# Two-layer diffusion backbone on one core: the modulation vectors of a half step are summed over the partitions in one pair of products at its end

## Chip, cores and metric

One Trainium2 chip, one of its cores. The metric is device time of one execution in microseconds (us); a difference is told against the runs of the kernel before on the same chip.

## What is computed

A two-layer block over 512 latent tokens and 256 context tokens of width 1024. Each layer is a half-step FFN, a token mixer (windowed attention in layer 0, Fourier mixing in layer 1), and a second half-step FFN. Every sub-layer is modulated by three vectors (shift, scale, gate) that come from a conditioning vector `c` through a large matrix. The part of the reference that matters:

```python
def modulate(x, mod, j):
    shift, scale = mod[:, 3 * j], mod[:, 3 * j + 1]
    return x * (1 + scale[:, None, :]) + shift[:, None, :]

def post_norm_update(x, y, mod, j, g, b):
    gate = mod[:, 3 * j + 2][:, None, :]
    return layer_norm(ALPHA * x + gate * y, g, b)

def half_ffn_sublayer(x, mod, j, wi, wo, g, b):
    y = 0.5 * swiglu(modulate(x, mod, j), wi, wo)
    return post_norm_update(x, y, mod, j, g, b)

mod_lat = (silu(c) @ mod_w[i] + mod_b[i]).reshape(-1, 9, D_MODEL)      # latent stream
mod_ctx = (silu(c_ctx) @ mod_w[i] + mod_b[i]).reshape(1, 9, D_MODEL)   # context stream
```

So nine vectors of 1024 for each layer and stream; vector 3j is the shift, 3j+1 the scale, 3j+2 the gate of sub-layer j. All arithmetic is fp32 in effect.

## The kernel before, in words

**Products.** Each fp32 factor is split into two parts of the fast fp32 format, high and low: ScalarE copies the high part (`wh`, `uh`, `hh`), VectorE subtracts to get the low one (`wl`, `ul`, `hl`). A product is then three matmuls (`mm3`: high-high, low-high, high-low).

**A half step** (`half_step`) has two stages. In the *up* stage (`ffn_up`) 22 pairs p = 0..21 are worked through; pair p computes two 128-row halves, `up` for the gate (silu on ScalarE: `sg`) and `up` for the value (VectorE multiplies: `u`). For 512 tokens a pair is 48 matmuls of 512 columns, for the 256 context tokens 48 of 256. In the *down* stage (`project`) the 22 rows of the down weights are worked through, f = 0..21; for each f four token tiles of six matmuls into `y`. There are eight PSUM banks, taken in turn: a pair takes two, a token tile of `y` two, a modulation product (`mp`) one. Five half steps run: 1 latent, 2 context (both layer 0, before attention), 3 latent (layer 0, after attention), 4 latent (layer 1, before the Fourier mixer), 5 latent (layer 1, after it).

**The gate** of a half step is folded into its down weights: `wr<-wr,gr` on VectorE multiplies each raw row block by `gr`, the gate as a row broadcast to all partitions. `gate_row` makes it, called from `late()` ahead of pair 20: ScalarE scales the column form (`gs`), its queue issues a DMA that writes it to DRAM as 1024 single numbers (`there`, called *the scatter* below) and, when that has landed, a DMA that reads it back broadcast (`gr`, called *the fetch*). Both stand in ScalarE's own instruction stream, which goes on behind the fetch only when the scatter has landed.

**The modulation vectors** beyond the first two are made beside the up stages of half steps 1 to 4 on VectorE: for each vector and stream eight steps `acc<-mr,silu_c,acc` over row blocks `mr` of the matrix, then `mod_fold`: a 32x32 transpose and a reduction that leave 128 partial sums in 32 columns. `mod_reduce` sums these over the partitions: one fp32 matmul with the constant `folder` into `mp`, and four small adds of the bias into `mod`. It is called for each vector a few steps after its fold (MOD_LAG), and for what is left in `mod_finish`, behind pair 19. Half step 1 makes the vectors shift/scale/gate 0 of the context, gate 0 of the latents, and 3 and 4 of both (8 products), half step 2 vectors 5 to 7 (3), half step 3 vector 8 (its own gate) and 0 to 3 of layer 1 (5), half step 4 vectors 4 to 8 of layer 1 (5; vector 5 is the Fourier mixer's gate, fetched in the same `late()` as the half step's own).

**What sets the order.** TensorE's and GpSimd's instructions stay in program order. VectorE's, ScalarE's and the DMA queue's (SP) are ordered by a scheduler when the kernel is built, except in stretches that are pinned; once built, each engine's stream is fixed. Raw weights come over SP, all through 42 SBUF slots. Completion of DMAs is counted on eight counters in turn, SP's and ScalarE's together: a DMA on a counter waits for the one eight before it.

Of the kernel before, what the change touches and what calls it, by code (L numbers as in the profile page):

```python
# [10 lines left out]
F32 = mybir.dt.float32  # L11
F32R = mybir.dt.float32r
AF = mybir.ActivationFunctionType
ALU = mybir.AluOpType

P = 128
D = 1024
KC = D // P
BLK = 32
# [29 lines left out]
P_WIDTH = 648  # L49
CORE_FETCH = 6  # L50
CORE_TILES = 5
MOD_LAG = 3
MOD_EARLY = 1
TURN_ACT = 4
BETWEEN = 5
# [49 lines left out]
class Emitter:  # L105
# [110 lines left out]
    def mod_fold(self, l, v, s, a):  # L216


        nc = self.nc
        turned = self.slot([P, 1024], F32, "mt")  # L220
        nc.vector.transpose(turned, a)
        t = self.small([P, D // BLK], "mr")
        nc.vector.tensor_reduce(
            out=t, in_=turned.rearrange("p (c k) -> p c k", k=BLK), axis=mybir.AxisListType.X, op=ALU.add
        )
        return l, v, s, t

    def mod_reduce(self, l, v, s, t):
        nc = self.nc
        ps = self.bank(nm="mp")  # L230
        self.mm(ps[:, : D // BLK], self.folder, t, start=True, stop=True)
        per = P // BLK
        for q in range(per):
            rows = slice(q * BLK, (q + 1) * BLK)
            cols = slice(v * KC, (v + 1) * KC)
            nc.vector.tensor_tensor(
                self.mod[l][s][rows, cols], ps[rows, q : D // BLK : per], self.mod_b[l][rows, cols], ALU.add
            )

    def mod_steps(self, n, ahead=2):  # L240
        nc = self.nc
        for _ in range(n):
            if self.n_job >= len(self.jobs):
                break
            while self.n_mraw < min(self.n_job + ahead + 1, len(self.jobs)):
                l, v, _, k = self.jobs[self.n_mraw]
                r = self.slot([P, 1024], F32, "mr")
                nc.sync.dma_start(r, self.ins["mod_w"][l, v, k])
                self.mraw[self.n_mraw] = r
                self.n_mraw += 1  # L250
            l, v, streams, k = self.jobs[self.n_job]
            r = self.mraw.pop(self.n_job)
            self.n_job += 1
            while self.due and self.due[0][0] <= self.n_job:
                self.mod_reduce(*self.due.pop(0)[1])
            for s in streams:
                sc = self.silu_c[:, s, k : k + 1]
                if k == 0:
                    a = self.slot([P, 1024], F32, "acc")
                    self.acc[s] = a  # L260
                    nc.vector.tensor_scalar(a, r, sc, None, ALU.mult)
                else:
                    a = self.acc[s]
                    nc.vector.scalar_tensor_tensor(a, r, sc, a, ALU.mult, ALU.add)
                if k == KC - 1:
                    self.due.append((self.n_job + MOD_LAG, self.mod_fold(l, v, s, self.acc.pop(s))))

    def mod_finish(self, upto):
        if upto > self.n_job:
            self.mod_steps(upto - self.n_job)  # L270
        while self.due:
            self.mod_reduce(*self.due.pop(0)[1])

    def col(self, l, s, v):
        return self.mod[l][s][:, v * KC : (v + 1) * KC]
# [492 lines left out]
    def run(self):  # L768
        nc = self.nc
        ins = self.ins  # L770
        sync = nc.sync
# [40 lines left out]

        h, held = self.head()
        sync.dma_start(self.mod_b[1], ins["mod_b"][1])
        self.folder = self.const([P, P], F32, "folder")
        sync.dma_start(self.folder, ins["folder"])
        self.ln_g = self.const([P, 6 * KC], F32, "ln_g")
        self.ln_b = self.const([P, 6 * KC], F32, "ln_b")
        sync.dma_start(self.ln_g, ins["ln_g_col"])
# [1 line left out]
        x = []  # L821
# [627 lines left out]
```

## Time and profile before

| | us |
|---|---|
| runs | 1991.20 median of 3 (1990.84 to 1992.42) |
| profiled execution | 1992.59, of it span 1990.8 |
| TensorE busy | 1971.8 (99% of the span), 10124 matmuls |
| VectorE busy | 1277.0 (64%) |
| ScalarE busy | 681.2 (34%) |
| DMA | 296.27 MB, mean 149 GB/s |

The page gives the busy time of each engine over the span; the chain gives, followed back from the last instruction, who was waited for. Busy times here mix stages: what a wait costs is read in the stage where it stands. In rows of the timeline the first number is the start, the second the length of a piece, `x2` how many like instructions are merged, and the bracket at the end the idle time before it and what ended that.

### The profile page before, as it was taken

The page shows a single profiled execution, that of the slowest core. Times are in us where ns is not written, and L with a number is a line of the kernel's source. Part 1 is how long each engine was busy: PE and PEld are TensorE (multiplying, and loading weights), DVE is VectorE, ACT ScalarE, POOL GpSimd, SP SyncE. Part 2 cuts the span into 40 slices and gives each one's busy share as a digit, 9 for nine tenths or more (in the row PEclk, how much of TensorE's full clock was granted, in tenths as well). Part 3 has the DMA queues.
Part 4 walks back from the last instruction along what each step waited for, and adds up shares of the span by engine and source line. Part 5 has one row for each costly group of instructions (what it writes and reads, how often), then busy time and mean ns, then how long its engine had stood idle before and what let it go on. Part 6 is the DMA issues. An engine that isn't in the chain of part 4 may idle for free.

```text
span 1990.8 us, 25353 instructions
## 1 busy us (share of the span) xinstructions
PE 1971.8 (99%) x10124; PEld 1674.7 (84%) x10124; DVE 1277.0 (64%) x1713; ACT 681.2 (34%) x991; POOL 73.4 (4%) x138
## 2 busy tenths in 40 slices
PE   8999999999999999999999999999999999999998
PEld 7888888899888887988888888888888988888886
DVE  6569985598756775766658455664766873333744
ACT  3322243334533685422224232222333632212320
POOL 0000000000000460000000000000000000000000
PEclk9999999999999999999999999999999999999999
DMA  9756543388732013455543326554441333232411
GB/s 377 262 185 206 185 150 131 116 297 297 254 101 73 10 45 107 159 190 196 195 149 123 120 98 225 195 191 138 140 135 64 110 98 117 90 94 87 138 64 43
DMA packets 90198, 296.27 MB, mean 149 GB/s; under 512 B 17248, under 2 KB 17504, under 8 KB 90080
## 3 DMA queue, kind: packets, MB, share of 16 engines
q1 hardware_dynamic: 81792, 290.96, 43.0%
q10 hardware_dynamic: 8288, 3.70, 0.7%
q8 instruction: 79, 1.29, 0.3%
q14 instruction: 39, 0.32, 0.1%
HBM read 292.50 MB, written 2.13 MB: 148 GB/s over the span
## 4 chain that ended last, share of the span: by engine, by line
PE 96%; DVE 2%; DMA 1%; ACT 1%; issue 0%; DVEq 0%; POOL 0%; SPq 0%; ACTq 0%; POOLq 0%
PE up L72 54%; PE y L72 30%; PE qkv L72 4%; PE s L72 2%; PE pt L72 2%; PE o L72 1%; PE tp L72 1%; DVE wl L72 1%; DVE x L72 0%; PE ab L72 0%; DMA wr<-in_wi_head_dram 0%; PE qt L72 0%; DVE ul L72 0%; PE f L72 0%; DMA ln_b<-in_ln_b_col_dram 0%
## 5 line engine op out<-in xcount | busy, mean ns | idle before, releaser
L72 DVE TENSOR_TENSOR wl<-wr,wh 128x1024 fp32r<-128x1024 f32 (+1 forms) x359 | 429.1, 1217 | 90.9 <-ACT wh L72 55.3
L72 ACT CAST wh<-wr 128x1024 fp32r<-128x1024 f32 (+1 forms) x364 | 368.5, 1046 | 218.2 <-PE y L72 92.5
L72 PE MATMUL up<-hh,wh 128*128 128x512 f32 (+1 forms) x1152 | 429.6, 373 | 0.0
L72 PE MATMUL up<-hl,wh 128*128 128x512 f32 (+1 forms) x1152 | 428.3, 372 | 0.0
L72 PE MATMUL up<-hh,wl 128*128 128x512 f32 (+1 forms) x1152 | 428.1, 372 | 0.0
L72 PE MATMUL y<-wh,uh 128*128 128x512 f32 x920 | 302.7, 390 | 1.4 <-DVE oT L72 1.4
L72 ACT ACTIVATE sg<-up 128x512 f32<-128x512 f32 (+1 forms) x110 | 61.1, 555 | 703.5 <-PE up L72 703.5
L72 PE MATMUL y<-wh,ul 128*128 128x512 f32 x920 | 301.8, 389 | 0.0
L72 PE MATMUL y<-wl,uh 128*128 128x512 f32 x920 | 301.6, 389 | 0.0
L72 DVE TENSOR_TENSOR u<-up,sg 128x512 f32<-128x512 f32 (+1 forms) x110 | 70.1, 637 | 335.0 <-PE up L72 334.6
L72 PEld LDWEIGHTS up<-hl,wh 128*128 128x128 f32 x1152 | 217.1, 188 | 37.5
L72 PEld LDWEIGHTS up<-hh,wl 128*128 128x128 f32 x1152 | 217.2, 189 | 37.2
L72 PEld LDWEIGHTS up<-hh,wh 128*128 128x128 f32 x1152 | 217.2, 189 | 36.9
L72 PEld LDWEIGHTS y<-wh,uh 128*128 128x128 f32 x920 | 172.6, 188 | 37.1 <-DVE oT L72 1.8
L72 PEld LDWEIGHTS y<-wh,ul 128*128 128x128 f32 x920 | 172.8, 188 | 35.9
L72 PEld LDWEIGHTS y<-wl,uh 128*128 128x128 f32 x920 | 172.8, 188 | 35.5
L72 DVE SCALAR_TENSOR_TENSOR acc<-mr,silu_c,acc 128x1024 f32<-128x1024 f32 x147 | 186.1, 1280 | 1.4
L72 DVE TENSOR_TENSOR wr<-wr,gr 128x1024 f32<-128x1024 f32 x99 | 120.5, 1238 | 41.4 <-DMA wr<-in_wo_dram 22.3
L72 PE MATMUL up<-h0h,wh 128*128 128x512 f32 x352 | 139.1, 398 | 0.2 <-ACT h0h L72 0.2
L72 PE MATMUL up<-h0l,wh 128*128 128x512 f32 x352 | 136.4, 390 | 0.0
L72 PE MATMUL up<-h0h,wl 128*128 128x512 f32 x352 | 136.2, 390 | 0.0
L72 PE MATMUL up<-chh,wh 128*128 128x256 f32 x352 | 100.1, 284 | 0.0
(171 smaller groups left out, 2143.0 us busy)
## 6 DMA issues: line engine op xcount, KB each, us to landing
wr<-in_wi_dram SPq DMA_DIRECT2D x213, 512.0 KB, 4.4
mr<-in_mod_w_dram SPq DMA_DIRECT2D x144, 512.0 KB, 4.1
wr<-in_wo_dram SPq DMA_DIRECT2D x110, 512.0 KB, 3.9
m<-in_mod_head_dram SPq DMA_DIRECT2D x16, 512.0 KB, 8.1
wr<-in_wqkv_dram SPq DMA_DIRECT2D x12, 512.0 KB, 3.6
wr<-in_attn_wo_dram SPq DMA_DIRECT2D x8, 512.0 KB, 3.5
wr<-in_fourier_wo_dram SPq DMA_DIRECT2D x8, 512.0 KB, 3.5
wr<-in_wi_head_dram SPq DMA_DIRECT2D x8, 448.0 KB, 9.6
```

Source lines behind the costliest of these rows:

```text
L72: ins = f(*args, **kw)
```

## The change

The vectors of a half step are no longer summed over the partitions one by one. Each fold writes its partial sums into a common tile `sums`; behind pair 19 one call splits the whole tile into high and low (`mp`, 32 columns for each vector: 256, 96, 160 and 160 columns in half steps 1 to 4), two matmuls with `folder`, now in the fast fp32 format, add both parts up, and the bias is added for runs of neighbouring vectors at once. So 21 products of one vector become 4 times 2, and 84 bias adds 28. `MOD_LAG` goes. `folder` is loaded into a slot and copied by ScalarE.

```diff
-MOD_LAG = 3
+MOD_MOST = 8
...
         nc.vector.transpose(turned, a)
-        t = self.small([P, D // BLK], "mr")
+        if not self.due:
+            self.sums = self.pool.tile([P, MOD_MOST, D // BLK], F32, tag="sums", name=self.name("sums"), bufs=1)
         nc.vector.tensor_reduce(
-            out=t, in_=turned.rearrange("p (c k) -> p c k", k=BLK), axis=mybir.AxisListType.X, op=ALU.add
+            out=self.sums[:, len(self.due)], in_=turned.rearrange("p (c k) -> p c k", k=BLK),
+            axis=mybir.AxisListType.X, op=ALU.add,
         )
-        return l, v, s, t
-
-    def mod_reduce(self, l, v, s, t):
+        self.due.append((l, s, v))
+
+    def mod_reduce(self):
+        if not self.due:
+            return
         nc = self.nc
-        ps = self.bank(nm="mp")
-        self.mm(ps[:, : D // BLK], self.folder, t, start=True, stop=True)
+        n = len(self.due)
+        cols = D // BLK
+        parts = self.slot([P, 2, MOD_MOST, cols], F32R, "mp")
+        self.split(parts[:, 0, :n], parts[:, 1, :n], self.sums[:, :n])
+        ps = self.bank(nm="mp")[:, : n * cols]
+        for i in range(2):
+            self.mm(ps, self.folder, parts[:, i, :n].rearrange("p n c -> p (n c)"), start=i == 0, stop=i == 1)
...
-            nc.vector.tensor_tensor(
-                self.mod[l][s][rows, cols], ps[rows, q : D // BLK : per], self.mod_b[l][rows, cols], ALU.add
-            )
+                nc.vector.tensor_tensor(dst, ps[rows, i : i + (m - 1) * step + 1 : step, q:cols:per], b, ALU.add)
...
-            while self.due and self.due[0][0] <= self.n_job:
-                self.mod_reduce(*self.due.pop(0)[1])
...
-                    self.due.append((self.n_job + MOD_LAG, self.mod_fold(l, v, s, self.acc.pop(s))))
+                    self.mod_fold(l, v, s, self.acc.pop(s))
...
-        while self.due:
-            self.mod_reduce(*self.due.pop(0)[1])
+        self.mod_reduce()
...
-        self.folder = self.const([P, P], F32, "folder")
-        sync.dma_start(self.folder, ins["folder"])
+        folder = self.slot([P, P], F32, "folder")
+        sync.dma_start(folder, ins["folder"])
+        self.folder = self.const([P, P], F32R, "folder")
+        nc.scalar.copy(self.folder, folder)
```

What this does to the order, shown at half step 3. First ScalarE around the making of the gate row, before (`sg_9006`, `sg_9081` and `sg_9164` belong to pairs 18, 19 and 20):

```order
L72 ACTIVATE sg_9006<-up_8943 128x512
L72 ACTIVATE gs_9090<-mod_0_90 128x8
L72 DMA there_9092<-gs_9090 128x8x1
L72 CAST wh_9023<-wr_8945 128x1024
L72 CAST wh_9053<-wr_8975 128x1024
L72 ACTIVATE sg_9081<-up_9019 128x512
L72 DMA gr_9094<-there_9092 128x1024
L72 CAST uh_9096<-u_7717 128x1024
L72 CAST wh_9104<-wr_9021 128x1024
L72 CAST wh_9135<-wr_9051 128x1024
L72 ACTIVATE sg_9164<-up_9100 128x512
```

And the same place now (`sg_9008` is pair 19's, `sg_9099` pair 20's; `wh_9039` is the last block of up weights, `wh_9070` the first of the down weights):

```order
L72 ACTIVATE sg_9008<-up_8946 128x512
L72 CAST mp_9011<-sums_7837 128x160
L72 ACTIVATE gs_9025<-mod_0_90 128x8
L72 DMA there_9027<-gs_9025 128x8x1
L72 DMA gr_9029<-there_9027 128x1024
L72 CAST uh_9031<-u_7672 128x1024
L72 CAST wh_9039<-wr_8948 128x1024
L72 CAST wh_9070<-wr_8978 128x1024
L72 ACTIVATE sg_9099<-up_9035 128x512
```

The scatter has moved from ahead of pair 19's silu to behind the product of all five vectors, and the fetch stands right behind it, where before two copies and a silu stood between. Half step 1 has the same order now; in half step 4 the half step's own scatter stands at the start of the up stage, its fetch behind `CAST mp`, and the Fourier gate's scatter and fetch stand one behind the other as above.

VectorE behind the product of half step 3, now, to the second `u` of the last two pairs (rows in the middle left out in two places):

```order
L72 TENSOR_TENSOR ul_9032<-u_7672,uh_9031 128x1024
L72 TENSOR_TENSOR wl_9040<-wr_8948,wh_9039 128x1024
L72 TENSOR_TENSOR wr_8978<-wr_8978,gr_9029 128x1024
L72 TENSOR_TENSOR wr_9037<-wr_9037,gr_9029 128x1024
L72 TENSOR_TENSOR wl_9071<-wr_8978,wh_9070 128x1024
L72 TENSOR_TENSOR u_9098<-up_9036,sg_9099 128x512
...
L72 TENSOR_TENSOR wl_9221<-wr_9135,wh_9220 128x1024
L72 TENSOR_TENSOR wr_9178<-wr_9178,gr_9029 128x1024
L72 TENSOR_TENSOR wr_9217<-wr_9217,gr_9029 128x1024
L72 TENSOR_TENSOR u_9098<-up_9103,sg_9166 128x512
```

From the first `wr<-wr,gr`, which needs the fetch, to pair 21's `u` (the last row) stand 12 operations of 1024 columns (multiplies by the gate row and splits) and two `u`. In half step 1 there are eight and two. Before, nearly the same rows stood there in nearly the same order; what moved is the fetch that they wait for.

TensorE at the start of that down stage, now, with the semaphores that each row waits for: `y_9201` and `y_9202` take the banks of pair 20, `y_9209` and `y_9210` those of pair 21.

```order
L72 MATMUL y_9185<-wh_9070,uh_9031 128x512 [waits Activation_49]
L72 MATMUL y_9186<-wh_9070,uh_9031 128x512
L72 MATMUL y_9185<-wl_9071,uh_9031 128x512 [waits DVE_49]
...
L72 MATMUL y_9201<-wh_9070,uh_9031 128x512 [waits Activation_49]
L72 MATMUL y_9202<-wh_9070,uh_9031 128x512 [waits DVE_49]
...
L72 MATMUL y_9209<-wh_9070,uh_9031 128x512 [waits Activation_49]
L72 MATMUL y_9210<-wh_9070,uh_9031 128x512 [waits DVE_49]
```

`y_9210` is the 20th matmul of the down stage and waits for VectorE: for pair 21's `u`, which reads the bank that `y_9210` takes. TensorE's own order around it is as before.

In half step 2 the context gate's scatter has moved the other way, from the end of the up stage to its start. There VectorE has pair 19's `u` ahead of the split of `mp`, in the other three half steps behind it.

On SP the load of `folder` has moved from the 16th DMA of the queue to the 40th, out of the loads that feed the head of the program; nothing else moved there.

More of the change, by code (lines that the diff above doesn't have):

```diff
@@ L229, in mod_reduce @@
+        self.due.append((l, s, v))
+    def mod_reduce(self):
+        if not self.due:
+            return
         nc = self.nc
-        ps = self.bank(nm="mp")
-        self.mm(ps[:, : D // BLK], self.folder, t, start=True, stop=True)
-        per = P // BLK
-        for q in range(per):
-            rows = slice(q * BLK, (q + 1) * BLK)
-            cols = slice(v * KC, (v + 1) * KC)
-            nc.vector.tensor_tensor(
-                self.mod[l][s][rows, cols], ps[rows, q : D // BLK : per], self.mod_b[l][rows, cols], ALU.add
-            )
+        n = len(self.due)
[5 more added lines that the diff above has]
+            self.mm(ps, self.folder, parts[:, i, :n].rearrange("p n c -> p (n c)"), start=i == 0, stop=i == 1)
+        ps = ps.rearrange("p (n c) -> p n c", c=cols)
+        per = P // BLK
+        at = {e: i for i, e in enumerate(self.due)}
+        todo = sorted(self.due)
+        self.due = []
+        while todo:
+            l, s, v = todo[0]
+            i = at[todo[0]]
+            m, step = 1, 1
+            while m < len(todo) and todo[m] == (l, s, v + m) and (m == 1 or at[todo[m]] == i + m * step):
+                if m == 1:
+                    step = at[todo[1]] - i
+                m += 1
+            todo = todo[m:]
+            for q in range(per):
+                rows = slice(q * BLK, (q + 1) * BLK)
+                dst, b = (
+                    x[rows, v * KC : (v + m) * KC].rearrange("p (n k) -> p n k", k=KC)
+                    for x in (self.mod[l][s], self.mod_b[l])
+                )
+                nc.vector.tensor_tensor(dst, ps[rows, i : i + (m - 1) * step + 1 : step, q:cols:per], b, ALU.add)
```

## The prediction

> **What bounds the kernel.** First the busy times and the chain of the page, by engine:
>
> ```profile
> PE 1971.8 (99%) x10124; PEld 1674.7 (84%) x10124; DVE 1277.0 (64%) x1713; ACT 681.2 (34%) x991; POOL 73.4 (4%) x138
> PE 96%; DVE 2%; DMA 1%; ACT 1%; issue 0%; DVEq 0%; POOL 0%; SPq 0%; ACTq 0%; POOLq 0%
> ```
>
> TensorE never rests, so a matmul that goes is a gain in full, and a wait that TensorE has to sit out is a loss in full. Everything else counts only if it makes TensorE wait. Two questions follow: what do the 21 small products cost, and does the later gate reach TensorE? For the second, how long the gate row takes. These are the landing times of the scatter (first row, seven of them) and those of the fetch with it in a second answer, the wait on ScalarE, and DMA shares around the scatter issued at 227.1:
>
> ```profile
> DMA to landing us min/median/max: 9.6/12.2/12.8
> DMA to landing us min/median/max: 3.6/6.5/8.1
> ACT uh L72 <- DMA there<-gs: 10.4, 2, 6.1
> 230.00:235.00 5.00, 5.00 (x24) 4.14 (x23) 5.00 (x6) 0.00 (x0) 0.00 (x0) 1.00 0.22 26
> 235.00:240.00 5.00, 5.00 (x24) 4.14 (x23) 5.00 (x5) 0.60 (x1) 0.00 (x0) 1.00 0.66 34
> 245.00:250.00 5.00, 5.00 (x24) 4.14 (x23) 3.45 (x4) 0.95 (x1) 0.00 (x0) 1.00 1.02 409
> ```
>
> The second row is the fetch: the gate needs 12.2 + 6.5 = 18.7 us from its vector to its row (median of each). ScalarE does stand still until the scatter lands, 10.4 us in two places. And while a scatter is out, loads hardly move: 26 and 34 GB/s against 409 (last number).
>
> **The products (gain).** TensorE's rows around one of them:
>
> ```profile
> 108.31 0.39 PE L72 MATMUL up<-h0h,wl 128*128 128x512 f32 x1
> 109.21 0.40 PE L72 MATMUL up<-h0l,wh 128*128 128x512 f32 x1
> 109.45 0.30 PE L72 MATMUL mp<-mr,folder 128*128 128x32 f32 x2
> 110.37 0.40 PE L72 MATMUL up<-h0h,wh 128*128 128x512 f32 x1
> 502.56 0.28 PE L72 MATMUL up<-chl,wh 128*128 128x256 f32 x1
> ```
>
> Four starts take 0.90 us from 108.31 to 109.21 (0.225 each) and 1.16 with the product between (109.21 to 110.37): 0.26 us a product, 21 make 5.5. The eight new matmuls have 96 to 256 columns in the fast format. The nearest row is the context's 128x256, which starts 0.12 us ahead of the next matmul (502.68, below): 8 x 0.12 = 1.0. From above, each costs what an old product did: 2.1. Gain 4.5, ends 3.4 and 5.5; I take 4.5, since the format is that of the nearest row.
>
> **The gate row (loss).** Take T as the start of the product behind pair 19. Half step 3 before, TensorE, VectorE and ScalarE:
>
> ```profile
> 1038.17 0.30 PE L72 MATMUL mp<-mr,folder 128*128 128x32 f32 x2
> 1038.37 0.69 DVE L72 TENSOR_TENSOR u<-up,sg 128x512 f32<-128x512 f32 x1 [1.52 <-PE up L72]
> 1038.97 0.68 DVE L72 TENSOR_TENSOR mod<-mp,mod_b 32x8 f32<-32x8 f32 x4
> 1040.19 3.50 DVE L72 TENSOR_TENSOR wr<-wr,gr 128x1024 f32<-128x1024 f32 x3 [0.54 <-DMA gr<-there]
> 1061.07 0.68 DVE L72 TENSOR_TENSOR u<-up,sg 128x512 f32<-128x512 f32 x1
> 1044.08 0.60 ACT L72 ACTIVATE sg<-up 128x512 f32<-128x512 f32 x1 [1.57 <-PE up L72]
> 1054.96 0.60 ACT L72 ACTIVATE sg<-up 128x512 f32<-128x512 f32 x1 [8.40 <-PE up L72]
> ```
>
> One pair is 10.88 us (1044.08 to 1054.96). Two pairs end at T + 0.25 + 21.76 = T + 22.0; 19 matmuls of the down stage later, at T + 26.3, TensorE starts the 20th, the one that takes the bank of pair 21's `u` (last rows of the order above). Before, the gate row was there at T + 2.0 (1040.19) and that `u` ended at 1061.75 = T + 23.6: 2.7 us to spare. That is the whole cover, and nothing of it shows as a wait in the page.
>
> After: `u` of pair 19 and four bias adds end at T + 1.5 (as in the rows: 1038.37, 1038.97 and 0.68), `gs` 0.2 more, scatter issued T + 1.75, landed T + 14.0, fetch landed T + 20.5. Behind it VectorE works off its stream. The step of one such operation is 1.14 us, from half step 4 (where before, ScalarE waited for the scatters too):
>
> ```profile
> 1398.22 0.60 ACT L72 ACTIVATE sg<-up 128x512 f32<-128x512 f32 x1 [8.20 <-PE up L72]
> 1402.24 0.82 ACTq L72 DMA_DIRECT2D gr<-there  x2
> 1403.10 1.05 ACT L72 CAST uh<-u 128x1024 fp32r<-128x1024 f32 x1 [4.29 <-DMA there<-gs]
> 1403.46 0.30 PE L72 MATMUL mp<-mr,folder 128*128 128x32 f32 x2
> 1421.93 2.36 DVE L72 TENSOR_TENSOR wl<-wr,wh 128x1024 fp32r<-128x1024 f32 x2
> 1424.21 2.36 DVE L72 TENSOR_TENSOR wr<-wr,gr 128x1024 f32<-128x1024 f32 x2
> 1426.48 0.69 DVE L72 TENSOR_TENSOR u<-up,sg 128x512 f32<-128x512 f32 x1
> ```
>
> (four operations from 1421.93 to 1426.48). The three places:
>
> - Half step 3: 12 operations and two `u` of 0.62: 14.9 us, `u` done at T + 35.4, TensorE's wait 35.4 - 26.3 = 9.1.
> - Half step 1: same times, 8 operations and two `u`, 10.4 us: T + 30.9, wait 4.6.
> - Half step 4: the own scatter is long home; its fetch goes behind `CAST mp` at T - 4.4 (1398.22 + 0.60 and a cast of some 0.3) and lands T + 2.1. VectorE's stream has the first `wr<-wr,gr` ahead of pair 19's `u`: 3.3, with `u` 3.9, adds 4.6, `gs` 4.8. The Fourier gate's scatter then holds ScalarE until T + 17.0. Queued behind it are `uh`, the last up weights, the first down weights and pair 20's silu; so VectorE gets `uh` at T + 18.4 (0.38 and 1.05 later) and has 13 operations and two `u`, 16.1 us: T + 34.5, wait 8.2.
>
> In all three the last up block also comes late (its split at T + 17.5 to 20.7, wanted at T + 16.8), but this shorter wait lies inside the longer one. The bounds come from the scatter (9.6 to 12.8), the fetch (3.6 to 8.1). At the low ends half step 1 waits 0, half step 3 3.6, half step 4 2.5; at the high ends 6.8, 11.3 and 10.4. I take the medians.
>
> **Half step 2 (loss).** The split of `mp` on VectorE stands behind pair 19's `u`, and TensorE's second product needs it.
>
> ```profile
> 502.68 0.30 PE L72 MATMUL mp<-mr,folder 128*128 128x32 f32 x2
> 502.95 0.42 DVE L72 TENSOR_TENSOR u<-up,sg 128x256 f32<-128x256 f32 x1 [0.66 <-PE up L72]
> ```
>
> `u` ends 0.7 us behind the product's old place, a split of 96 columns is no longer than a 256-column `u` of 0.42: wait 0.9, from 0.7 (`u` alone) to 1.1. In the other half steps the split stands ahead of `u` and needs only the silu of the first half of pair 19 (1398.22, 5.2 us ahead of the product): nothing, covered by these 5.2 us.
>
> **The clock (loss).** TensorE would stand still about 9 us in half step 3. The one long idle time in this trace is the start:
>
> ```profile
> 6.70 1.84 PE L72 MATMUL ms<-silu_c,m 128*128 128x1 f32 x8 [6.70 <-DMA m<-in_mod_head_dram]
> 11.60 3.55 PE L72 MATMUL up<-h0h,wh 128*128 128x512 f32 x7
> 14.94 1.83 PE L72 MATMUL up<-h0h,wl 128*128 128x512 f32 x7
> ```
>
> After 6.7 us without work, seven matmuls took 3.55 us, the next seven 1.83. So a wait over 6.7 us may cost 1.7 more; I charge it once, for half step 3 (bounds: never, and at all three, 5.1). [...]
>
> **At nothing.** The 56 adds saved are VectorE time (0.16 us each), and VectorE is at 64%. `folder` leaves the head's loads; TensorE is the one waited for there from 11.60 on, so no gain. Its cast (under 1 us) falls near 60 us, ahead of weight copies with 7 us of idle time behind them:
>
> ```profile
> 71.56 0.60 ACT L72 ACTIVATE sg<-up 128x512 f32<-128x512 f32 x1 [7.38 <-PE up L72]
> 392.03 1.64 SPq L182 DMA_DIRECT2D wr<-in_wi_dram  x2
> 407.69 1.99 ACT L72 CAST wh<-wr 128x1024 fp32r<-128x1024 f32 x2
> ```
>
> The scatters that go early (start of the up stages of half steps 2 and 4) stop the loads for some 10 us; SP's next load on the same counter waits for them too, and all SP loads behind it. In half step 2 a block issued at 392.03 was wanted at 407.69, 15.7 us later, against 12.2 us of stop and some 4 of loading, and a split block has a further pair ahead of TensorE: covered, narrowly. If not, each microsecond beyond is TensorE's; the price is up to 10 us. SP also holds the latent inputs `x` behind half step 1's scatter; they are wanted only after the down stage.
>
> **Sum.** -4.5 + 9.1 + 4.6 + 8.2 + 0.9 + 1.7 = +20.0 us on the profiled 1992.6 (span 1990.8), 2012.6; on the median of the runs, 1.4 lower than the profiled one, 1991.2 + 20.0 = **2011.2**. About 4.0 us (0.2%) can be told from no change.
>
> **Rivals.**
>
> - *Only the weights are late.* If the banks didn't bind (another bank free, or `u` earlier), TensorE would wait just for the splits: in half steps 1 and 3 for the first down block, three operations behind the fetch, T + 24.0 against T + 22.5 where its low part is wanted, 1.5 each; in half step 4 for the last up block, T + 20.7 against T + 16.8, 4.0. Sum -4.5 + 7.0 + 0.9 = +3.4: 1994.6. Against it: the order's wait of `y_9210` on VectorE. It turns on whether pair 21's `u` ends before T + 26.3. Chance 0.08.
> - *The late gate is hidden (the other side).* If scatter and fetch together take under 8 us behind T, VectorE's 14.9 us end within T + 26.3 and only the gain and half step 2 are left: -3.6, 1987.6, no change by the bound above. Against it: no scatter under 9.6 in seven. [...] Chance 0.04.
> - *The early scatters starve the up stages.* As forecast, and in half step 2 the stop of 10 us outruns the loads' lead: +10, 2021. For it, 26 GB/s beside a scatter; against it, the 15.7 us of lead. Chance 0.08.
>
> **Chances.** The forecast has 0.80, its own range 2003 to 2019 (its low ends together give -5.5 + 6.1 + 0.7 = +1.3, its high ends -3.4 + 28.5 + 1.1 + 5.1 = +31, neither likely in all places at once). The range for eight in ten is 2001 to 2022, with most of the starving case. Slower by over 0.2%: 0.87 (forecast, starving, a little of the first rival less the forecast's low end); within: 0.11; faster: 0.02.
>
> **What would show it.** In the profile after: TensorE waiting for VectorE or ScalarE at `y` in half steps 1, 3 and 4, some 5, 9 and 8 us, with `u` as what ended the longest; ScalarE waiting some 12 us for the scatter three times, at about T + 2 to T + 14; VectorE waiting for the fetch in half steps 1 and 3; a `mp` that waits about 0.9 us in half step 2 alone; matmuls of 0.5 us behind a long wait if the clock fell. I am wrong if `y` shows no wait (then the banks or the scatter's time are misread), or if `up` waits for loads early in half step 2.

## The result, and the profile after

Before: 1991.6 us, median of 4 runs. Changed: **2011.2 us**, median of 4 (2008.9 to 2013.7). The ratio is 1.0098 (95% interval 1.0085 to 1.0110): about 20 us slower; the forecast was 2011.2 us. The profiled execution took 2012.6 us, its span is 2010.8 us. The total came out as forecast; the terms did not all do so, and that is the main matter below.

First the page after (busy times, and the chain by engine), then the waits of TensorE that the kernel before does not have:

```profile
PE 1976.3 (98%) x10090; PEld 1675.9 (83%) x10090; DVE 1270.0 (63%) x1661; ACT 681.8 (34%) x996; POOL 73.4 (4%) x138
PE 91%; DVE 4%; DMA 3%; issue 1%; ACT 1%; SPq 0%; DVEq 0%; POOL 0%; ACTq 0%; POOLq 0%
```

```profile
PE y L72 <- DVE u L72: 11.8, 3, 6.3
PE up L72 <- ACT wh L72: 2.0, 1, 2.0
PE up L72 <- DVE wl L72: 1.6, 2, 0.9
PE mp L72 <- DVE mp L72: 0.7, 1, 0.7
```

TensorE's share of the chain falls from 96% to 91%; the scatters and fetches (DMA) and VectorE take it. The waits are where they were forecast: three times at `y`, ended by `u`; at `up` for the last block of weights; and once at `mp`. Together they are 16.1 us, and 16.1 less 4.5 for the products is 11.6, not 20. What is missing is in no wait.

Apart from the products both kernels run the same 10082 matmuls in the same order, so each matmul of the one can be set beside the same matmul of the other. The lag of after behind before, in us:

| place | lag ahead of it | step there |
|---|---|---|
| the head of the program | 0 | -0.7 |
| half step 1: products; wait at `y`; matmuls behind it | -0.71 | -1.78; +3.06; +1.74 |
| half step 2: products; wait at `mp` | +2.32 | -0.43; +0.91 |
| half step 3: products; waits at `up`, `y`; matmuls behind | +2.83 | -1.15; +0.93, +6.49; +2.71 |
| half step 4: products; waits at `up`; matmuls behind; wait at `y`; matmuls behind | +11.81 | -1.16; +3.39; +1.65; +2.77; +1.52 |
| end | +19.97 | +20.0 in all |

Sums: products -4.5, waits +17.5, slower matmuls behind waits +7.6, head -0.7. (A lag counts the whole gap; the list of waits leaves out its edges, so 17.5 and not 16.1.) The last kind is the missing part. Half step 3, whose products start at T = 1039.89: ScalarE's and VectorE's rows, then TensorE's:

```profile
1041.64 0.38 ACTq L72 DMA_DIRECT2D there<-gs  x1
1053.95 1.05 ACT L72 CAST uh<-u 128x1024 fp32r<-128x1024 f32 x1 [12.34 <-DMA there<-gs]
1058.30 2.36 DVE L72 TENSOR_TENSOR wr<-wr,gr 128x1024 f32<-128x1024 f32 x2 [0.91 <-DMA gr<-there]
1060.64 1.23 DVE L72 TENSOR_TENSOR wl<-wr,wh 128x1024 fp32r<-128x1024 f32 x1
1061.90 0.69 DVE L72 TENSOR_TENSOR u<-up,sg 128x512 f32<-128x512 f32 x1
...
1070.60 2.35 DVE L72 TENSOR_TENSOR wr<-wr,gr 128x1024 f32<-128x1024 f32 x2
1072.86 0.69 DVE L72 TENSOR_TENSOR u<-up,sg 128x512 f32<-128x512 f32 x1
```

```profile
1073.61 0.80 PE L72 MATMUL y<-wh,uh 128*128 128x512 f32 x1 [6.32 <-DVE u L72]
1074.20 1.06 PE L72 MATMUL y<-wl,uh 128*128 128x512 f32 x2
...
1079.25 0.62 PE L72 MATMUL y<-wl,uh 128*128 128x512 f32 x2
```

Read down: the scatter holds ScalarE for 12.3 us; VectorE waits for the fetch until T + 18.4; then pair 21's `u` stands behind twelve operations and ends at 1073.55; TensorE's matmul for that bank starts 0.06 us later. Behind the wait two matmuls take 1.06 us instead of 0.62. Cut into pieces of 3.41 us, as long as the half clock lasted there, the stretch around half step 1's wait reads (PE busy is the second number, the granted clock the third from the end):

```profile
263.36:266.77 3.41, 2.44 (x11) 1.69 (x9) 3.41 (x4) 1.55 (x2) 0.00 (x0) 1.00 0.82 315
266.77:270.19 3.42, 1.49 (x6) 1.24 (x7) 3.42 (x5) 2.09 (x2) 0.00 (x0) 1.00 0.16 18
270.19:273.60 3.41, 3.41 (x9) 2.63 (x8) 3.38 (x4) 1.46 (x2) 0.00 (x0) 0.50 0.35 136
273.60:277.01 3.41, 3.41 (x16) 2.82 (x15) 3.41 (x4) 1.49 (x2) 0.00 (x0) 1.00 0.32 107
```

A wait of 2.9 us, spread over two such pieces, left the second 57% idle; the next one ran at half clock with TensorE busy throughout, nine matmul starts instead of sixteen. That is 1.7 us lost after the wait is over. A fall of the clock stands behind the waits in half steps 3 and 4 too, and costs 1.5 to 2.7 us each time.

### The profile page after: what moved, and what is told of

Same layout as the page of the kernel before. It is cut to its first block, busy times and chain, and to the rows that moved or that the text cites. A ratio compares the mean times of both kernels' runs of the same rounds, so it can differ in the third digit from the quotient of the medians.

```text
span 2010.8 us, 25214 instructions
## 1 busy us (share of the span) xinstructions
PE 1976.3 (98%) x10090; PEld 1675.9 (83%) x10090; DVE 1270.0 (63%) x1661; ACT 681.8 (34%) x996; POOL 73.4 (4%) x138
## 4 chain that ended last, share of the span: by engine, by line
PE 91%; DVE 4%; DMA 3%; issue 1%; ACT 1%; SPq 0%; DVEq 0%; POOL 0%; ACTq 0%; POOLq 0%
PE up L72 50%; PE y L72 29%; PE qkv L72 4%; PE s L72 2%; DMA there<-gs 2%; PE pt L72 2%; PE o L72 1%; DVE wr L72 1%; DVE wl L72 1%; PE tp L72 1%; DMA gr<-there 1%; DVE x L72 0%; PE ab L72 0%; PE qt L72 0%; DMA wr<-in_wi_head_dram 0%
```

## Experiments

Two theories stood beside each other. *The late gate*: the own gate row comes late, pair 21's `u` waits in VectorE's queue behind what needs it, and the clock falls behind TensorE's waits. *The form*: the collecting, the split or the wide products cost something of their own. Times of before in these series: 1991.6 to 1992.2 us.

**Where the products stand: undone alone, and done alone.** `own_early` is the changed kernel with three vectors taken out of the wait for pair 19:

```diff
+OWN = ((0, 0, 2), (0, 0, 8), (1, 0, 5))
+OWN_LAG = 4
...
+            if self.flush is not None and self.flush <= self.n_job:
+                self.flush = None
+                self.mod_reduce()
...
                     self.mod_fold(l, v, s, self.acc.pop(s))
+                    if (l, s, v) in OWN:
+                        self.flush = self.n_job + OWN_LAG
```

Each triple in `OWN` is layer, stream, vector.

> The changed kernel, but the three gate vectors that are used in the half step that makes them (gate 0 and vector 8 of layer 0, vector 5 of layer 1) are summed with whatever has been collected four matrix steps behind their fold, and the rest behind pair 19: 7 pairs of products instead of 4. Theory 1 (the late own gate is the whole loss): the waits at y and up in half steps 1, 3 and 4 go and the clock stays up, which takes back the 4.8 + 10.1 + 9.3 us by which those places lag in the changed kernel's trace; three more pairs of products at about 0.3 cost 0.9: 2011.2 - 24.2 + 0.9 = 1987.9 us, 0.998 of before. Theory 2 (the collecting or the split as such costs): most of the loss stays, above 2005 us.

`gates_late` is the kernel before with those three held back and everything else as it was:

```diff
-                    self.due.append((self.n_job + MOD_LAG, self.mod_fold(l, v, s, self.acc.pop(s))))
+                    at = self.kept if (l, s, v) in OWN else self.due
+                    at.append((self.n_job + MOD_LAG, self.mod_fold(l, v, s, self.acc.pop(s))))
...
     def mod_finish(self, upto):
...
+        self.due += self.kept
+        self.kept = []
```

> The kernel before, single fp32 products, with one thing moved: the three gate vectors that are used in the half step that makes them are summed behind pair 19, as in the changed kernel; all others stay where they were. Theory 1: the loss comes with the gates alone: +4.8 in half step 1, +10.1 in half step 3, +9.3 in half step 4, no gain from products: 1991.6 + 24.2 = 2015.8 us, 1.012 of before, with waits at y for u, and the clock falling in all three. Theory 2 (the split, the wide products or the joint adds cost): about 1992 us.

Measured: own_early 1991.3 us, ratio 0.9998 (0.9989 to 1.0007); gates_late 2014.3 us, 1.0113 (1.0099 to 1.0127). Moving three of 21 products, with no change of form, costs 22 us, most of the 25 that waits and clock cost in the changed kernel (17.5 + 7.6); moving these three back takes 20 us away. The waits of gates_late that before does not have:

```profile
PE y L73 <- DVE u L73: 10.8, 3, 5.5
PE up L73 <- ACT wh L73: 3.1, 1, 3.1
PE up L73 <- DVE wl L73: 1.9, 2, 0.9
```

They stand at the same places, and are ended by the same engines, as those of the changed kernel. So the form is not the loss. But own_early lacks 3.4 us of what was expected; that is taken up below. And gates_late came out 1.5 us under its expectation, mostly because in half step 1 the clock did not fall:

```profile
265.05:268.46 3.41, 2.15 (x10) 1.45 (x8) 3.41 (x4) 1.47 (x3) 0.00 (x0) 1.00 0.40 126
268.46:271.88 3.42, 1.94 (x8) 1.61 (x9) 3.42 (x4) 1.81 (x2) 0.00 (x0) 1.00 0.60 190
271.88:275.29 3.41, 3.41 (x16) 2.82 (x15) 3.37 (x4) 1.92 (x3) 0.00 (x0) 1.00 0.25 99
```

Nearly the same wait (2.7 us of idle time against 2.9), but it fell on two pieces almost evenly, neither over 43% idle.

**What TensorE waits for: the bank or the weights.** `u_first` leaves the gate as late as it is and only shortens VectorE's queue ahead of `u`:

```diff
+U_AHEAD = 1
...
-                w_hi, w_lo = self.weights(pairs[p][half])
+                at = pairs[p][half]
+                w_hi, w_lo = self.weights(at, ahead=min(SPLIT_AHEAD, pairs[-1][1] + U_AHEAD - at))
```

> The changed kernel with the gate row as late as there (scatter home about T + 13, fetch about T + 19), but in pairs 20 and 21 the down weights are prepared only one block ahead, so VectorE has four to six operations instead of 8 to 12 between the fetch and pair 21's u. Theory 1 (TensorE waits for a bank that VectorE's queue holds): u ends at about T + 24.5 in half step 1 and T + 26.5 in half step 3, against T + 26.3 wanted, so the waits at y and the clock's falls behind them go: -4.8 in half step 1, -9.2 in half step 3 (0.9 at up stays), -4.3 in half step 4 (the 3.4 at up and one fall of the clock stay): 2011.2 - 18.3 = 1992.9 us, about level with before. Theory 2 (the late down weights are what is waited for): the wait moves to the first down blocks, y waiting for wl, by some 3 us and more in half steps 1 and 3, and the time stays above 2003 us.

Measured: 1992.2 us, 1.0001 (0.9993 to 1.0010). VectorE in half step 3 (T = 1037.5), and TensorE's waits over the whole span that before does not have:

```profile
1054.71 2.36 DVE L73 TENSOR_TENSOR wr<-wr,gr 128x1024 f32<-128x1024 f32 x2 [0.54 <-DMA gr<-there]
1057.06 1.23 DVE L73 TENSOR_TENSOR wl<-wr,wh 128x1024 fp32r<-128x1024 f32 x1
1058.31 0.69 DVE L73 TENSOR_TENSOR u<-up,sg 128x512 f32<-128x512 f32 x1
1058.92 2.35 DVE L73 TENSOR_TENSOR wr<-wr,gr 128x1024 f32<-128x1024 f32 x2
1061.19 1.22 DVE L73 TENSOR_TENSOR wl<-wr,wh 128x1024 fp32r<-128x1024 f32 x1
1062.32 0.68 DVE L73 TENSOR_TENSOR u<-up,sg 128x512 f32<-128x512 f32 x1
```

```profile
PE y L73 <- DVE ul L73: 1.8, 2, 1.2
PE up L73 <- DVE wl L73: 0.7, 1, 0.7
PE mp L73 <- DVE mp L73: 0.7, 1, 0.7
```

The fetch is there at T + 17.2, nearly as late as in the changed kernel (T + 18.4), yet `u` ends at T + 25.5, and no `y` waits for `u` any more; the clock stays up (0.999 over the span, as in before). The wait was for the bank. The weights do come late too, a little: `ul`, queued behind the same work, costs 1.8 us. The total was hit in part by chance: of the 3.4 us at `up` in half step 4 that were expected to stay, 0.9 stayed (why, stands under half step 4 below).

**The clock.** `warm` adds matmuls whose result is overwritten, just ahead of token tile 3's first `y`:

```diff
+                    if (f, t, i, half) == (0, 3, 0, 0):
+                        for _ in range(self.warm_y.get(w0, 0)):
+                            mm(y[:, cs], s[:, sl], w[:, cs], start=True, stop=True)
...
+        self.warm_y = {w_l0[1]: 12, w_l1[1]: 27, w_l2[1]: 11}
```

> The changed kernel; TensorE does the same matmul of token tile 3 (its first y bank, where the result is begun anew each time) 12, 27 and 11 times more in half steps 1, 3 and 4, just where it would wait for pair 21's u: some 2.7, 6.1 and 2.5 us of work in waits of 3.1, 6.5 and 2.8. Nothing else moves. Theory 1 (half clock is the price of TensorE's idle time): no half clock in half steps 1 and 3 and one stretch less in half step 4: -1.6 - 2.7 - 1.5 = -5.8, 2005.4 us. Theory 2 (the slow matmuls behind a wait have another cause, the end of a wait or late operands): no change, 2011.2 us.

Measured: 2006.2 us, 1.0072 (1.0059 to 1.0086): 50 matmuls more, 5.0 us less. The intervals of the two kernels just touch (the changed one's begins at 1.0085), so the traces carry this point. The same stretch of half step 3 in the changed kernel and in warm:

```profile
1065.00:1080.00 15.00, 8.68 (x28) 6.67 (x27) 14.97 (x14) 7.15 (x8) 0.00 (x0) 0.77 0.29 105
```

```profile
1065.00:1080.00 15.00, 15.00 (x68) 12.43 (x67) 14.96 (x14) 7.87 (x8) 0.00 (x0) 1.00 0.24 88
```

The granted clock goes from 0.77 to 1.00, and nothing but what TensorE does in those waits was changed. So the half clock here follows from idle time. (In half step 4 the fall at `up` stayed away as well, 1.00 from 1430 to 1440 against 0.83, though no matmul was added there: the waits were 1.1 and 1.0 us in this execution, against 2.0 and 0.9.)

**Half step 4.** `fourier_later` moves the second gate row:

```diff
         def late():
...
-            if more is not None:
-                self.fold(self.gate_row(*more[0], 1.0), more[1], KC)
             stat(0)
...
         def middle():
...
+            if more is not None:
+                self.fold(self.gate_row(*more[0], 1.0), more[1], KC)
```

> The changed kernel; the Fourier mixer's gate row is made in the down stage of half step 4 instead of its late call, so that its scatter does not stand in ScalarE's stream ahead of the last up weights. Half steps 1 to 3 stay. Theory 1 (half step 4 loses because ScalarE is held by that scatter): all of half step 4's lag goes, 3.4 at up, 2.8 at y and 3.2 of clock: 2011.2 - 9.3 = 2001.9 us. Theory 2 (half step 4's own fetch, which lands at about T + 2, is late for VectorE too): the wait at up goes, that at y stays: about 2006 us.

Measured: 2002.5 us, 1.0051 (1.0039 to 1.0064). In half step 4 TensorE no longer waits at all; its lag stays at 9.35 us from the last `up` to the end, where the changed kernel goes from 10.65 to 19.97. So that half step lost because the other gate's scatter held ScalarE. The changed kernel's rows there (T = 1414.15), VectorE's first, then ScalarE's:

```profile
1416.48 1.23 DVE L72 TENSOR_TENSOR wr<-wr,gr 128x1024 f32<-128x1024 f32 x1 [6.41 <-DMA gr<-there]
1419.31 0.38 ACTq L72 DMA_DIRECT2D there<-gs  x1
1430.83 1.04 ACT L72 CAST uh<-u 128x1024 fp32r<-128x1024 f32 x1 [11.55 <-DMA there<-gs]
```

The half step's own fetch is not out of it, though: it sets when that scatter can start. The bias adds, which the scatter's vector needs, stand on VectorE behind this `wr<-wr,gr`, and it waits for the own fetch. It started at T + 2.3 in the changed kernel, T + 1.7 in warm, T + 0.5 in u_first and T - 0.1 in one_fp32; the scatter was issued at T + 5.2, 4.5, 3.3 and 2.7, and TensorE's lag at `up` grew by 3.4, 2.5, 0.9 and 1.0 us.

**The split.** `one_fp32` drops it, with `folder` left in fp32:

```diff
-        parts = self.slot([P, 2, MOD_MOST, cols], F32R, "mp")
-        self.split(parts[:, 0, :n], parts[:, 1, :n], self.sums[:, :n])
...
-        for i in range(2):
-            self.mm(ps, self.folder, parts[:, i, :n].rearrange("p n c -> p (n c)"), start=i == 0, stop=i == 1)
+        self.mm(ps, self.folder, self.sums[:, :n].rearrange("p n c -> p (n c)"), start=True, stop=True)
```

> The changed kernel without the split: the vectors of a half step are collected and summed behind pair 19 by one fp32 product of 256, 96, 160 and 160 columns. Theory 1 (the late gate is the loss, the split is not): waits and clock as in the changed kernel, except half step 2's 0.9 for the split; one fp32 product of 32 columns cost 0.26, so four wide ones cost between 4 x 0.26 = 1.0 and 21 x 0.26 = 5.5, against 1.2 for the eight fast ones: 2010 to 2014.6 us. Theory 2 (the split and its waits carry the loss): below 2000 us.

Measured: 2007.4 us, 1.0077 (1.0064 to 1.0091), 2.6 us under the range. The loss stays, as theory 1 says. The low end was missed for three reasons that its trace shows: in half step 1 the wait was 1.9 us and the clock held (1.2 less, and no half clock); in half step 4 its own fetch landed sooner (T - 0.1, above), so the lag there grew by 7.8 and not 9.3; and the wide fp32 products are cheap. Rows of one_fp32, then of the changed kernel:

```profile
238.63 0.40 PE L72 MATMUL up<-h0l,wh 128*128 128x512 f32 x1
238.86 0.59 PE L72 MATMUL mp<-sums,folder 128*128 128x256 f32 x2
239.10 0.59 PE L72 MATMUL up<-h0h,wh 128*128 128x512 f32 x1
239.53 0.40 PE L72 MATMUL up<-h0h,wl 128*128 128x512 f32 x1
```

```profile
239.06 0.40 PE L72 MATMUL up<-h0l,wh 128*128 128x512 f32 x1
239.30 0.40 PE L72 MATMUL mp<-mp,folder 128*128 128x256 f32 x2
239.53 0.40 PE L72 MATMUL up<-h0h,wh 128*128 128x512 f32 x1
```

Starts are 0.227 us apart without a product. One fp32 product of 256 columns adds 0.90 - 2 x 0.227 = 0.45 us; two fast ones add 0.47 - 0.23 = 0.24. The split saves 0.2 us here and costs a wait of 0.9 in half step 2. By the account of the table above the products gained about 4.1 us in one_fp32, against 4.5. So nearly all of the gain comes from joining the products, not from the format.

**A version that keeps the gain.** `pair_early` is the changed kernel with one number altered, so that all collecting ends one pair earlier:

```diff
-MOD_EARLY = 1
+MOD_EARLY = 2
```

> The changed kernel with the collecting ended one pair earlier: the products stand behind pair 18. Everything stays collected and split. Theory 1 (late gate against a cover of 2.7 us): one pair is 10.9 us, more than the longest lag of 10.1, so the waits at y and up and the clock's falls go in all three half steps: 2011.2 - 24.2 = 1987.0 us, 0.998 of before; half step 2's wait of 0.9 may stay. Theory 2 (the collecting, the split or the early scatters cost): above 2005 us. Theory 3 (VectorE gets short of time when a half step's matrix steps are packed into 18 pairs): waits of TensorE for wl or u in the up stages, some 1990 to 2000 us.

Measured: 1995.2 us, 1.0016 (1.0007 to 1.0025): the gate's waits are gone, as expected, and 8 us are lost elsewhere. The time lies in the range of theory 3, but its waits, for `wl` or `u` in the up stages, are not there. Where the time goes shows at the product of half step 1, and likewise in own_early (first pair_early's TensorE, then own_early's TensorE and VectorE):

```profile
230.68 0.54 PE L72 MATMUL mp<-mp,folder 128*128 128x256 f32 x1 [2.38 <-DVE mp L72]
```

```profile
185.33 0.33 PE L74 MATMUL mp<-mp,folder 128*128 128x128 f32 x1 [1.34 <-DVE mp L74]
184.39 0.68 DVE L74 TENSOR_TENSOR u<-up,sg 128x512 f32<-128x512 f32 x1
184.99 0.28 DVE L74 TENSOR_TENSOR mp<-sums,mp 128x128 fp32r<-128x128 f32 x1
```

TensorE has come to its product and waits for a split (0.28 us long in own_early) that stands behind a `u`: the half step 2 wait of the changed kernel, now in other half steps too. In pair_early one such wait (3.3 us of lag) brought the clock down: the matmuls of `up` behind it start 0.43 us apart, ahead of it 0.23. Two cures were run on own_early, and one of them on pair_early: split each vector right behind its fold (own_split, below), or do without the split, by the edit of one_fp32 (own_fp32, pair_fp32).

```diff
+        t = a[:, : D // BLK]
         nc.vector.tensor_reduce(
-            out=self.sums[:, len(self.due)], in_=turned.rearrange("p (c k) -> p c k", k=BLK),
-            axis=mybir.AxisListType.X, op=ALU.add,
+            out=t, in_=turned.rearrange("p (c k) -> p c k", k=BLK), axis=mybir.AxisListType.X, op=ALU.add
         )
+        n = len(self.due)
+        self.split(self.sums[:, 0, n], self.sums[:, 1, n], t)
...
-        parts = self.slot([P, 2, MOD_MOST, cols], F32R, "mp")
-        self.split(parts[:, 0, :n], parts[:, 1, :n], self.sums[:, :n])
+        parts = self.sums
```

> As own_early, but each vector is split into high and low right behind its fold, so that the split no longer stands in VectorE's queue at the moment TensorE comes to the product. Theory 1 (what own_early lacks, 1991.3 against 1987.9 us, is TensorE waiting for the low part: 1.7, 0.9 and 1.3 us at the products of half steps 1, 2 and 3): these waits go, 1991.3 - 3.9 = 1987.4 us, 0.998 of before. Theory 2 (it is something else, or the 21 small splits delay VectorE): 1990 us or more.

> As own_early, with one fp32 product in place of the split and the two fast ones (7 products). Theory 1 (the split is worth nothing to TensorE: in one_fp32 a 256-column fp32 product added 0.45 us, the two fast ones of the changed kernel 0.24, and the split's own wait cost 0.9 in half step 2): the waits of own_early (3.9 us) go, the products cost some 0.1 more each: 1991.3 - 3.9 + 0.7 = 1988.1 us, level with own_split's 1988.0. Theory 2 (the split is needed for the gain): 1990 us or more.

> As pair_early (all vectors of a half step summed behind pair 18), with one fp32 product for each half step in place of the split and the two fast ones. Theory 1 (pair_early's 8 us above expectation are the split's low part, which stands in VectorE's queue behind two wl and a u when TensorE comes to it: waits of 3.3 with a fall of the clock, 1.1, 1.4 and 1.4): these waits go, four products cost some 1.3 in all: 1995.2 - 1.6 - 3.3 - 1.1 - 1.4 - 1.4 + 0.6 = 1987.0 us, the best of all. Theory 2 (VectorE is short of time in 18 pairs, or the gate row is still late): 1990 us or more.

Measured: own_split 1988.0 us, 0.9980 (0.9971 to 0.9988); own_fp32 1988.4 us, 0.9983 (0.9974 to 0.9992); pair_fp32 **1987.5 us**, 0.9979 (0.9970 to 0.9988), each within 0.6 us of what theory 1 gives. In none of the three does TensorE wait for `mp`, `u`, `wh` or `wl`. All three are some 0.2% faster than the kernel before (none of the intervals reaches 1) and, by these intervals, can't be told from one another. The simplest is pair_fp32: collect, end one pair earlier, one fp32 product.

## Why the prediction was right, and where it was not

- *Products, -4.5 forecast, -4.5 measured.* The nearest row, a fast matmul of the context's width at 0.12 us, held: the two of half step 1 added 0.24.
- *Half step 2, +0.9 forecast, +0.91 measured*, by the mechanism named: the split behind pair 19's `u`.
- *Half step 1, wait 4.6 forecast, 3.1 measured; half step 3, 9.1 against 7.4 (6.5 at `y`, 0.9 at `up`).* The mechanism and VectorE's queue were right: from the first use of the fetch to the end of `u` 15.2 us in half step 3, forecast 14.9. The mis-sized term is the way of the gate row. Scatter and fetch were put at 12.2 + 6.5 = 18.7 us; from the scatter's issue to the first `wr<-wr,gr` it was 1058.30 - 1041.64 = 16.7 us in half step 3 and 16.9 in half step 1. The medians were taken over seven places of the kernel before.
- *Half step 4, 8.2 forecast, 3.4 at `up` and 2.8 at `y` measured.* Here the forecast put everything at `y`, with the shorter wait at `up` inside it. Of the two, `u` did end when forecast (T + 34.0 against T + 34.5), but the clock's fall behind `up` moved TensorE 1.65 us towards it: 3.4 + 1.65 + 2.8 = 7.8.
- *The clock, +1.7 forecast once, +7.6 measured in four falls.* This is the step that failed. It was drawn from the one long idle time in the trace of before, 6.7 us at the start, and so charged only half step 3; waits of 2.8 us were enough, and half step 3 alone cost 2.7. Nor did the sum follow its own condition, waits over 6.7 us: the 8.2 forecast for half step 4 meets it as well, and would have made the term 3.4. The bounds, "at all three, 5.1", did not hold it either.
- *The head, 0 forecast, -0.7.* TensorE's first work started 0.65 us earlier. That is not `folder` leaving the head: with it there (gates_late) the start was at 6.8 us, without it (fourier_later) at 7.1. What moves the start is not shown.
- *At nothing*: the early scatters in half steps 2 and 4 left no wait of `up` for a load, and the lag does not change there, though SP did stand still behind them (up to 14.1 us); that rival is out. So is the weights-only one (u_first). So is the hidden gate: the three scatters alone held ScalarE for over 11 us each. (The 8 us that the prediction allows scatter and fetch together there do not come out of its own terms: from the scatter's issue they are 26.3 - 14.9 - 1.75 = 9.65 in half step 3. Its low end for half step 4, 2.5, comes to 8.2 - 2.6 - 2.9 = 2.7. Neither changes what was forecast.)

So the total was hit because two errors nearly cancel: the waits were 5.3 us too high (22.8 forecast, 17.5 measured), the clock 5.9 too low. Only in half step 4 do they hang together. Place, order and sign were read right; the exact 2011.2 is luck, the more so as the four runs of the changed kernel spread over 4.8 us.

## What to carry to other kernels

When late work is batched, look for the one member of the batch that something needs at once, and follow what it delays through the in-order queues to the bank or buffer whose release the busiest engine needs: the cover was 2.7 us and stood in no list of waits, and three of 21 products decided the time. A short operation that an engine must wait for (here a split of 0.3 us) costs what stands ahead of it in its queue, so issue it where its input is made. And price a wait of a busy TensorE with what follows it: here 1.7 us more where it left 57% of a 3.4 us piece idle, and 2.7 where it ran on into the next piece.

## What was not expected of the hardware

Between its first and last 20 us the changed kernel's trace has four stretches with a granted clock of 0.50, from 270.19, 1072.32, 1434.13 and 1447.78 us on. Three are 3.413 us long, that of half step 3 twice as long (6.827 us), and the later three start 235, 341 and 345 such steps behind the first. Cutting this trace into pieces on that step: the four pieces at full clock in which TensorE was idle for 57, 62, 81 and 100% were each followed by a piece at half clock, and none of those with 47% or less. The one piece at half clock in which TensorE was still idle for 38% was followed by another, the other four, idle for 14% or less, by full clock; so half step 3, whose wait ran on into the half-clock piece, lost 2.7 us. And of two waits of 2.9 and 2.7 us one cost 1.7 more (half step 1 of the changed kernel, 57% of one piece) and one nothing (half step 1 of gates_late, 37% and 43% of two). What sets the step is not shown.
